# Expert weights of a three-block model, laid out as pairs of tiles and loaded 2 MB at a time in rows of 16 KB

## The chip, the cores and the metric

The kernel runs on one core of a Trainium2 chip. The metric is the device time of one execution in microseconds (us), taken as the median of several runs. A profile of one execution, with a trace of every instruction and of the DMA packets, was taken beside them.

## What is computed

The reference is three transformer-like blocks in a row over one sequence of 256 tokens of width 1024. The change concerns the last part of the third block, a feed-forward of 16 experts in which each expert chooses its 32 tokens:

```python
def expert_choice_ffn(h, w_router, w_gate, w_up, w_down):
    b, s, d = h.shape
    cap = EC_CAPACITY * s // N_EXPERTS          # 2 * 256 // 16 = 32
    affinity = jax.nn.softmax((h @ w_router).astype(jnp.float32), axis=-1)
    top_val, top_idx = lax.top_k(affinity.transpose(0, 2, 1), cap)
    xe = jax.vmap(lambda hb, ib: hb[ib])(h, top_idx)
    act = jax.nn.silu(jnp.einsum('becd,edf->becf', xe, w_gate)) * jnp.einsum('becd,edf->becf', xe, w_up)
    ye = jnp.einsum('becf,efd->becd', act, w_down) * top_val[..., None].astype(h.dtype)
    return jax.vmap(lambda yb, ib: jnp.zeros((s, d), yb.dtype).at[ib.reshape(-1)].add(yb.reshape(-1, d)))(ye, top_idx)
...
        x = x + expert_choice_ffn(rms_norm_3(x, norm_ffn_g[l]), w_router[l], w_exp_gate[l], w_exp_up[l], w_exp_down[l])
    return rms_norm_3(x, norm_final_g)
```

Each expert has a gate and an up matrix of 1024 x 2048 and a down matrix of 2048 x 1024, all float32: 8 MB each, 24 MB per expert, 384 MB in all, and each weight is used for 32 tokens only. The result is summed into the residual and normalized once more.

## The kernel before

Everything is float32 in memory. The first two blocks and most of the third (projections, two kinds of attention, recurrences) run in the first half of the time; their weights come through a ring of three places of 8 KB per partition (`ring`, `load_w`, L282), and each is split into a high and a low part (`wh` on ScalarE and `wl` on VectorE, places in the pool `hl`, `split_w`, L287 to L304) that TensorE multiplies in three products (L311 to L313 and L327 to L329). The residual stands in the pool `res`.

The experts (L1770) work on units of 1 MB: 128 partitions of 8 KB, two tiles of 128 x 1024. A unit of gate or up is 128 rows of the matrix of 2048 columns, so a partition reads one row of 8 KB; a unit of down is 256 rows of 1024 columns, so a partition reads two rows of 4 KB from places half a megabyte apart. `load` (L1876) gives each unit the next of 21 places in turn, issues the transfer on SyncE's queue (SP), and TensorE's matmuls for it follow: four with 512 columns for gate and up (L1902, into the PSUM tile `pgu`), four for down (L1974, into `pd`). The trace shows each such matmul as two instructions, so a unit is a group of 8. The 21 places are, in this order: 13 places in four pools `er0` to `er3` (3, 3, 5 and 2), which are opened one after the other as the third block gives up its memory (`slots`, L246, called at L1729, L1734, L1736 and L1752); the three of `ring`; three in `hl`, where a unit is two transfers of 0.5 MB with rows of 4 KB (`wwh` and `wwl`, L1890); two in `res`. So the first 21 units are on their way while the third block still ends: its last weights w_mg3a and w_mg3b (merging the branches) and w_out3 (output projection) go through the same SP queue, in which the experts' loads stand among them.

Between gate and up and down there are small steps per expert: silu and product (`gg`), four transposes (`pat`, `at`), the weighted one-hot (`pr`, `ppv`, `pvt`), and after down two copies (`ye`) and four matmuls that scatter the result into the residual (`pye`, L1922). The last expert's down is cut by output columns (`parts`: 512, 256, 256), so that norm and output of the first part run beside the loads of the next; its transfers are sixteen of 0.5 MB with rows of 2 KB and 1 KB (L1892). Before the first expert stand the router (L1797 to L1805), softmax, top-k by eight values at a time (L1844 to L1846), and the gathering of tokens by one-hot matmuls (`pxe`, L1861 to L1871), which is interleaved with the first expert's gate and up.

The order of instructions on each engine is set by a scheduling framework that places instructions by their dependences and priorities when the kernel is built; SP issues its transfers strictly in that order and waits at each until its place is free. Eight semaphores serve SP's transfers in turn, so that at most eight are in flight.

Of the kernel before, what the change touches and what calls it, by code (L numbers as in the profile page):

```python
# [10 lines left out]
F32 = mybir.dt.float32  # L11
# [5 lines left out]

S = 256
D = 1024
BIG = 1e30  # L20
EPS = 1e-6

# [141 lines left out]
def layout(x):  # L164
    x = {k: np.asarray(v) for k, v in x.items()}
    a = {}
    ca, coff = const_pack()
    a.update(ca)
    parts = vec_parts(x)
    voff, _ = offsets(parts)  # L170
    a["vecs"] = np.ascontiguousarray(np.concatenate([np.asarray(v, np.float32) for v in parts.values()], 1))
    xt = lambda t: np.ascontiguousarray(t.T.reshape(8, 128, S).transpose(1, 0, 2))
    a["x"] = xt(x["x"][0])
    a["mem"] = xt(x["mem_3"][0])
    a["w_ada"] = np.ascontiguousarray(x["w_ada"][0].T.reshape(12, 2, 128, D).transpose(0, 2, 1, 3)).reshape(12, 128, 2 * D)
    a["crow"] = x["c"]
    w = x["w_in"][0]
    a["w_in"] = wchunks(np.concatenate([w[:, :2048], w[:, 2056:]], 1), 256)
    a["w_ba"] = np.ascontiguousarray(w[:, 2048:2056].reshape(8, 128, 8).transpose(1, 0, 2))
    rows = lambda *names: wchunks(np.concatenate([x[k][0] for k in names], 0), 256)  # L180
    a["w_mg1"] = rows("w_proj_dn", "w_proj_mb")
    a["w_out"] = wchunks(x["w_out"][0], 256)
    w = x["w_in_2"][0]
    a["w_in2"] = wchunks(np.concatenate([w[:, :1536], w[:, 1544:]], 1), 256)
    a["w_if"] = np.ascontiguousarray(w[:, 1536:1544].reshape(8, 128, 8).transpose(1, 0, 2))
    a["lru_w"] = np.ascontiguousarray(np.stack([
        x["lru_wa_2"][0].reshape(2, 128, 64), x["lru_wx_2"][0].reshape(2, 128, 64)], 0).transpose(2, 0, 1, 3))
    a["w_mg2"] = rows("w_out_lru_2", "w_out_mlstm_2", "w_out_sb_2")
    a["w_o2"] = wchunks(x["w_o_2"][0], 256)
    w = x["w_ffn_in_2"][0]  # L190
    a["w_f1"] = np.ascontiguousarray(np.concatenate(
        [w[:, :2816].reshape(1024, 22, 1, 128), w[:, 2816:].reshape(1024, 22, 1, 128)], 2).reshape(1024, 5632))
    a["w_f1"] = wchunks(a["w_f1"], 256)
    w = x["w_ffn_out_2"][0]
    a["w_f2a"] = wchunks(w[:1024], 256)
    a["w_f2b"] = wchunks(w[1024:2048], 256)
    a["w_f2c"] = wchunks(w[2048:], 256)
    a["w_in3"] = wchunks(x["w_in_3"][0], 256)
    pad = np.zeros((6, 7, 127), x["na_rpb_3"].dtype)
    pad[:, :, 48:79] = x["na_rpb_3"][0, :, 4:11]  # L200
    a["rpb"] = np.stack([pad[:, :, 63 - c:127 - c] for c in range(64)], 0)
    a["lora"] = np.ascontiguousarray(np.concatenate([x["rw_w2_3"][0], x["rw_a2_3"][0]], 1).transpose(1, 0, 2))
    a["g2"] = x["rw_g2_3"][0]
    a["w_mkv"] = wchunks(x["w_mem_kv_3"][0], 256)
    a["w_mg3a"] = rows("w_branch_na_3", "w_branch_mem_3")
    a["w_mg3b"] = rows("w_branch_rw_3")
    a["w_out3"] = wchunks(x["w_out_3"][0], 256)
    a["w_rt"] = np.zeros((128, 8, 32), x["w_router_3"].dtype)
    a["w_rt"][:, :, :16] = x["w_router_3"][0].reshape(8, 128, 16).transpose(1, 0, 2)
    a["w_eg"] = x["w_exp_gate_3"][0]  # L210
    a["w_eu"] = x["w_exp_up_3"][0]
    a["w_ed"] = x["w_exp_down_3"][0]
    a["g_fin"] = x["norm_final_g_3"].reshape(1, 1024)
    return {k: np.ascontiguousarray(v) for k, v in a.items()}, coff, voff

ES = [3, 3, 5, 2]
RB = 3  # L220
PB = [3, 3, 2]
HP = None
HB = 3


class Core:
# [19 lines left out]
    def slots(self):  # L246

        n = len(self.er)
        self.er.append(self.ctx.enter_context(self.tc.tile_pool(name=f"er{n}", bufs=ES[n], side="right")))

    def load_vecs(self):
        self.nc.sync.dma_start(self.vt, self.A["vecs"])
# [398 lines left out]
def ada(K, pool):  # L651
# [7 lines left out]
    def part(c0, c1):  # L659
        for c in range(c0, c1):  # L660
            w = K.load_w(K.A["w_ada"][c], 2, D)
            for f in range(2):
# [1107 lines left out]
def experts(K, last, ep, tmp, pool, out):  # L1770

    nc, A, V, C, tc = K.nc, K.A, K.V, K.C, K.tc
# [43 lines left out]
    for t in range(2):  # L1816
        i = nc.scalar.activation(aff[:, t], zl[:, t], AF.Exp, scale=rs[:, t:t + 1], accum_out=su[:, t:t + 1])


    for t in range(2):  # L1820
        for k0 in (0, 4):
            p = K.psum([128, 4, 128], "ptm", "as"[t])
# [5 lines left out]
            else:  # L1828
                with tc.issue_after(i.ins):
                    nc.scalar.copy(d, p)  # L1830
                    nc.scalar.activation(hn[:, t], acc[:, t], AF.Copy, scale=rs[:, t:t + 1])
                    i = nc.scalar.copy(hh[:, t], hn[:, t])
# [37 lines left out]
        else:  # L1870
            nc.vector.tensor_scalar(d, p, V("g_ffn3", k), None, op0=ALU.mult)  # L1871

    slots = [p for p, n in zip(K.er, ES) for _ in range(n)] + [K.ring] * RB + [K.hl] * HB + [K.res] * 2
    cnt = [0]

    def load(src, g=None):  # L1876

        pool = slots[cnt[0] % len(slots)]
        cnt[0] += 1
        if pool is K.hl:  # L1880
            w = [pool.tile([128, 1024], F32, tag=t, name="w" + t) for t in ("wh", "wl")]
        else:
            w = pool.tile([128, 2, 1024], F32, tag="x" if pool is K.res else "w", name="w")
            if g is None:
                nc.sync.dma_start(w, src.rearrange("i p n -> p i n"))
                return w[:, 0], w[:, 1]
            w = w[:, 0], w[:, 1]
        for i in range(2):
            if g is None:
                nc.sync.dma_start(w[i], src[i])  # L1890
            else:
                nc.sync.dma_start(w[i].rearrange("p (g n) -> p g n", g=g), src[i].rearrange("g p n -> p g n"))  # L1892
        return w

    def up(src, e, before=None):
        pg = K.psum([128, 512], "pgu", "g")
        for k in range(8):
            if before is not None:
                before(k)
            w = load(src[e, k * 128:k * 128 + 128, :].rearrange("p (i n) -> i p n", i=2))  # L1900
            for j in range(4):
                nc.tensor.matmul(pg[32 * j:32 * j + 32], xe[:, k, e * 32:e * 32 + 32],  # L1902
                                 w[j // 2][:, j % 2 * 512:j % 2 * 512 + 512], start=k == 0, stop=k == 7)
        return pg
# [6 lines left out]
    def run(work):  # L1911
# [1 line left out]
        gr = work.tile([1, 1024], F32, name="gr")  # L1913
        sm = work.tile([128, 2, 3], F32, name="fsm")
        rs = work.tile([128, 2], F32, name="frs")
        parts = [(0, 512), (512, 768), (768, 1024)]

        def add(pvt, ye, c0, c1):

# [26 lines left out]
        for e in range(16):  # L1946
# [10 lines left out]
            last = nc.scalar.copy(at, pt)  # L1957
# [8 lines left out]
            ye = work.tile([128, 1024], F32, tag="ye", name="ye")  # L1966
            pd = [K.psum([128, 512], f"pd{i}") for i in range(2)]
            if e < 15:
                for c in range(8):
                    w = load(A["w_ed"][e, c * 256:c * 256 + 256, :].rearrange("(i p) n -> i p n", p=128))  # L1970
                    for i in range(2):
                        j, q = divmod(2 * c + i, 4)
                        for hh in range(2):
                            nc.tensor.matmul(pd[hh][32 * q:32 * q + 32], at[:, q, 32 * j:32 * j + 32],  # L1974
                                             w[i][:, hh * 512:hh * 512 + 512], start=j == 0, stop=j == 3)
                nc.scalar.copy(ye[:, 0:512], pd[0])  # L1976
                nc.vector.tensor_copy(ye[:, 512:1024], pd[1])  # L1977
                for c0 in (0, 512):
                    for _ in add(pvt, ye, c0, c0 + 512):
                        pass  # L1980
                continue
# [6 lines left out]
            for n, (c0, c1) in enumerate(parts):  # L1988
                m = c1 - c0
                g = 1024 // m  # L1990
                p = pd[c0 // 512][:, c0 % 512:c0 % 512 + m]
                for i in range(0, 16, 2 * g):
                    w = load(A["w_ed"][e, i * 128:(i + 2 * g) * 128, c0:c1].rearrange("(i g p) n -> i g p n", i=2, g=g), g)
                    for u in range(2 * g):
                        j, q = divmod(i + u, 4)
                        nc.tensor.matmul(p[32 * q:32 * q + 32], at[:, q, 32 * j:32 * j + 32],
                                         w[u // g][:, u % g * m:u % g * m + m], start=j == 0, stop=j == 3)
                h = c0 + m // 2
                nc.scalar.copy(ye[:, c0:h], p[:, 0:m // 2])
                nc.vector.tensor_copy(ye[:, h:c1], p[:, m // 2:])  # L2000
                for t, a in add(pvt, ye, c0, c1):
                    finish(t, n, a)
# [7 lines left out]
def body(ctx: ExitStack, tc: tile.TileContext, A, out, coff, voff):  # L2010
    nc = tc.nc
    K = Core(ctx, tc, A, coff, voff)
# [12 lines left out]
    with tc.tile_pool(name="b3", bufs=1) as pool:  # L2025
        last = block3(K, xt, pool, mem, norms)
        ep = ctx.enter_context(tc.tile_pool(name="ep", bufs=1, side="right"))
        with tc.tile_pool(name="et", bufs=1) as tmp:
            run = experts(K, last, ep, tmp, pool, out)
    with tc.tile_pool(name="ew", bufs=1) as work:  # L2030
        run(work)
    K.late.close()

# [14 lines left out]
```

## Time and profile before

| | |
|---|---|
| median of 3 runs | 1981.33 us (1977.47 to 1982.41) |
| the profiled execution | 1979.57 us |
| its span, first to last instruction | 1977.6 us |
| TensorE (PE), VectorE (DVE), ScalarE (ACT), GpSimd (POOL) busy | 1649.7, 771.7, 590.2, 106.8 us |
| DMA over the span | 557.04 MB in 106917 packets, mean 282 GB/s |
| the chain that ended last | PE 46%, DMA 41%, DVE 8% of the span |

The page of a profile gives busy time by engine, the span in 40 slices of 49.4 us with one digit per slice for the busy share in tenths, the rate of DMA in each slice, the chain of work that ended last (followed back from the last instruction through what released each step), the costliest groups of instructions, and the transfers. The trace answers narrower questions: tables of busy time by stretches, the waits of an engine and what ended them, and instructions in order of time. GB are 10^9 bytes; a MB of a weight unit is 2^20 bytes.

### The profile page before, as it was taken

The numbers are of one execution on the slowest core, as the hardware profiler recorded it, in microseconds if no ns is written. First come the engines' busy times: TensorE is split into PE (matmuls) and PEld (weight loads), VectorE is DVE, ScalarE is ACT, GpSimd is POOL, SyncE is SP. The second block draws the span as 40 slices with busy tenths as digits, with TensorE's granted clock in tenths as the row PEclk, the third lists the DMA queues.
The fourth block names the chain that finished last, engine by engine and source line by source line (L and its number), as shares of the span: only waits on it lengthen the run. The fifth ranks groups of instructions, "written<-read, shape, count | busy, mean of one in ns | idle before, by whom it ended". The sixth has DMA issues, their size and how long they took to land.

```text
span 1977.6 us, 28659 instructions
## 1 busy us (share of the span) xinstructions
PE 1649.7 (83%) x11882; PEld 1062.5 (54%) x11882; DVE 771.7 (39%) x1529; ACT 590.2 (30%) x1159; POOL 106.8 (5%) x123
## 2 busy tenths in 40 slices
PE   3999989999999999989979776677777677767776
PEld 2998989899999998868974111111111111111111
DVE  7797767657655676855571000000000000000001
ACT  3655555764554454633441000000000000000001
POOL 0000000000000121300020000000000000000000
PEclk9998989999999999979999888888878889777888
DMA  7442643344545553322689999999999999999998
GB/s 298 171 149 89 230 170 117 138 141 173 177 174 186 179 198 128 108 76 88 235 310 375 414 415 415 415 417 416 416 416 415 416 416 414 414 415 417 418 416 293
DMA packets 106917, 557.04 MB, mean 282 GB/s; under 512 B 10530, under 2 KB 17058, under 8 KB 61859
## 3 DMA queue, kind: packets, MB, share of 16 engines
q1 hardware_dynamic: 106786, 555.21, 72.1%
q8 instruction: 93, 1.52, 0.3%
q14 instruction: 38, 0.30, 0.0%
HBM read 554.12 MB, written 1.05 MB: 281 GB/s over the span
## 4 chain that ended last, share of the span: by engine, by line
PE 46%; DMA 41%; DVE 8%; ACT 2%; issue 1%; SPq 1%; POOL 1%; DVEq 0%; ACTq 0%
DMA w<-in_w_eg 15%; DMA w<-in_w_eu 13%; PE psg L313 10%; PE psg L311 10%; PE psg L312 10%; DMA w<-in_w_ed 5%; DMA wwl<-in_w_eu 4%; DVE wl L302 2%; PE pgu L1902 2%; PE pd L1974 2%; DMA wwh<-in_w_eu 1%; DVE w L664 1%; DMA wwl<-in_w_eg 1%; DMA wwh<-in_w_eg 1%; PE psg L328 1%
## 5 line engine op out<-in xcount | busy, mean ns | idle before, releaser
L1902 PE MATMUL pgu<-w,xe 128*32 128x512 f32 x1768 | 304.2, 782 | 155.1 <-DMA w<-in_w_eu 89.1
L302 DVE TENSOR_TENSOR wl<-w,wh 128x512 fp32r<-128x512 f32 (+1 forms) x510 | 330.6, 690 | 183.2 <-ACT wh L300 170.6
L300 ACT CAST wh<-w 128x512 fp32r<-128x512 f32 x516 | 287.7, 607 | 253.1 <-PE psg L312 223.3
L1902 PEld LDWEIGHTS pgu<-w,xe 128*32 128x32 f32 x1768 | 42.9, 121 | 393.6 <-DMA w<-in_w_eu 222.3
L1974 PE MATMUL pd<-w,at 128*32 128x512 f32 x808 | 186.0, 637 | 48.5 <-DMA w<-in_w_ed 43.0
L1952 DVE TENSOR_TENSOR gg<-gg,pgu 128x512 f32<-128x512 f32 x16 | 11.0, 688 | 503.9 <-PE pgu L1902 500.3
L1974 PEld LDWEIGHTS pd<-w,at 128*32 128x32 f32 x808 | 42.2, 115 | 183.5 <-DMA w<-in_w_ed 112.7
L1977 DVE COPY ye<-pd 128x512 f32<-128x512 f32 x15 | 10.4, 692 | 294.5 <-PE pd L1974 294.5
L313 PE MATMUL psg<-n3hh,wl 128*128 128x256 f32 x344 | 103.0, 299 | 3.2 <-POOL wl L302 1.7
L311 PE MATMUL psg<-h1h,wh 128*128 128x256 f32 x352 | 103.0, 293 | 0.0
L311 PE MATMUL psg<-n3hh,wh 128*128 128x256 f32 x344 | 101.5, 295 | 1.6 <-ACT wh L300 1.6
L313 PE MATMUL psg<-h1h,wl 128*128 128x256 f32 x352 | 102.2, 290 | 0.0
L312 PE MATMUL psg<-h1l,wh 128*128 128x256 f32 x352 | 101.7, 289 | 0.0
L1957 ACT COPY at<-pat 128x512 f32<-128x512 f32 x16 | 9.4, 585 | 308.6 <-PE pat L1955 297.1
L312 PE MATMUL psg<-n3hl,wh 128*128 128x256 f32 x344 | 100.8, 293 | 0.1
L312 PE MATMUL psg<-n2fhl,wh 128*128 128x256 f32 x352 | 100.0, 284 | 0.2
L313 PE MATMUL psg<-n2fhh,wl 128*128 128x256 f32 x352 | 99.8, 283 | 0.0
L311 PE MATMUL psg<-n2fhh,wh 128*128 128x256 f32 x352 | 99.6, 283 | 0.0
L1951 ACT ACTIVATE gg<-pgu 128x512 f32<-128x512 f32 x16 | 9.6, 597 | 277.3 <-PE pgu L1902 277.2
L311 PE MATMUL psg<-n2hh,wh 128*128 128x256 f32 x304 | 87.1, 287 | 2.0 <-ACT n2hh L453 2.0
L312 PE MATMUL psg<-n2hl,wh 128*128 128x256 f32 x304 | 87.7, 289 | 0.2 <-DVE n2hl L456 0.2
L1976 ACT COPY ye<-pd 128x512 f32<-128x512 f32 x15 | 8.8, 585 | 264.6 <-issue 257.3
(725 smaller groups left out, 3473.8 us busy)
## 6 DMA issues: line engine op xcount, KB each, us to landing
w<-in_w_eg SPq DMA_DIRECT2D x112, 1024.0 KB, 18.5
w<-in_w_eu SPq DMA_DIRECT2D x109, 1024.0 KB, 19.9
w<-in_w_ed SPq DMA_DIRECT2D x101, 1024.0 KB, 18.8
w<-in_w_in SPq DMA_DIRECT2D x68, 1024.0 KB, 4.8
w<-in_w_f SPq DMA_DIRECT2D x22, 1024.0 KB, 4.8
w<-in_w_ada SPq DMA_DIRECT2D x12, 1024.0 KB, 5.3
wwh<-in_w_ed SPq DMA_DIRECT2D x19, 512.0 KB, 14.7
wwl<-in_w_ed SPq DMA_DIRECT2D x19, 512.0 KB, 15.2
```

The lines of the kernel that those rows point to most:

```text
L300: self.nc.scalar.copy(wh[:, a:b], w[:, k0 + a:k0 + b])
L302: e.tensor_tensor(wl[:, a:b], w[:, k0 + a:k0 + b], wh[:, a:b], op=ALU.subtract)
L311: nc.tensor.matmul(out, a, x[0], start=first, stop=False)
L312: nc.tensor.matmul(out, a, x[1], start=False, stop=False)
L313: nc.tensor.matmul(out, b, x[0], start=False, stop=last)
L328: nc.tensor.matmul(out, xl[:, k, ts], wh[:, c0:c1], start=False, stop=False)
L664: nc.vector.scalar_tensor_tensor(w[:, f], w[:, f], 1.0, sg, op0=ALU.mult, op1=ALU.mult, accum_out=out[:, j:j + 1])
L1902: nc.tensor.matmul(pg[32 * j:32 * j + 32], xe[:, k, e * 32:e * 32 + 32], w[j // 2][:, j % 2 * 512:j % 2 * 512 + 512], start=k == 0, stop=k ...
L1951: nc.scalar.activation(gg, pgu[0], AF.Silu)
L1952: nc.vector.tensor_tensor(gg, gg, pgu[1], op=ALU.mult)
L1974: nc.tensor.matmul(pd[hh][32 * q:32 * q + 32], at[:, q, 32 * j:32 * j + 32], w[i][:, hh * 512:hh * 512 + 512], start=j == 0, stop=j == 3)
L1977: nc.vector.tensor_copy(ye[:, 512:1024], pd[1])
```

## The change

The host lays the expert weights out anew. Gate and up become blocks of 256 matrix rows in which each partition's two rows of 8 KB follow each other; down becomes blocks of 512 matrix rows in which each partition's four rows of 4 KB follow each other. A block is 2 MB, 16 KB per partition in one piece. The last expert's down is stored apart (`w_edl`), in eight blocks of 1 MB in the order in which its column parts use them, 8 KB per partition in one piece.

The places become eight of 16 KB and four of 8 KB, 20 MB: six pairs and one single in the `er` pools (whose sizes change from 3, 3, 5, 2 to 2, 4, 4, 3), the three singles of `ring`, and two pairs in a new pool `lw`, which is opened where `hl` and `res` stood, once both are closed (K.late.close() moves ahead of the experts' main part). A pair's place takes a block in one transfer with rows of 16 KB; two single places take a block in two transfers with rows of 8 KB. The matmuls are the same, in the same units. `load` becomes a generator that hands out one unit after the other.

```diff
+LAST = [(0, 512), (512, 768), (768, 1024)]
...
-    a["w_eg"] = x["w_exp_gate_3"][0]
-    a["w_eu"] = x["w_exp_up_3"][0]
-    a["w_ed"] = x["w_exp_down_3"][0]
+    for k, n in (("w_eg", "w_exp_gate_3"), ("w_eu", "w_exp_up_3")):
+        a[k] = x[n][0].reshape(16, 4, 2, 128, 2048).transpose(0, 1, 3, 2, 4)
+    w = x["w_exp_down_3"][0]
+    a["w_ed"] = w.reshape(16, 4, 4, 128, 1024).transpose(0, 1, 3, 2, 4).reshape(16, 4, 128, 2, 2048)
+    last = []
+    for c0, c1 in LAST:
+        g = 1024 // (c1 - c0)
+        last.append(w[15, :, c0:c1].reshape(8 // g, 2 * g, 128, c1 - c0).transpose(0, 2, 1, 3).reshape(8 // g, 128, 2048))
+    a["w_ed"] = a["w_ed"][:15]
+    a["w_edl"] = np.concatenate(last, 0)
...
-ES = [3, 3, 5, 2]
+ES = [2, 4, 4, 3]
...
-        self.er.append(self.ctx.enter_context(self.tc.tile_pool(name=f"er{n}", bufs=ES[n], side="right")))
+        if ES[n] % 2:
+            self.er1 = self.ctx.enter_context(self.tc.tile_pool(name="er", bufs=1, side="right"))
+        self.er.append(self.ctx.enter_context(self.tc.tile_pool(name=f"er{n}", bufs=ES[n] // 2, side="right")))
...
-    slots = [p for p, n in zip(K.er, ES) for _ in range(n)] + [K.ring] * RB + [K.hl] * HB + [K.res] * 2
+    slots = [(p, 2) for p, n in zip(K.er, ES) for _ in range(n // 2)] + [(K.er1, 1)] + [(K.ring, 1)] * RB + [(None, 2)] * 2
     cnt = [0]
 
-    def load(src, g=None):
...
+    def load(srcs):
+
+        for src in srcs:
+            two, i = len(src.shape) == 3, 0
+            while i < (2 if two else 1):
+                pool, n = slots[cnt[0] % len(slots)]
+                cnt[0] += 1
+                pool = pool or K.lw
+                if n == 2:
+                    w = pool.tile([128, 2, 2048], F32, tag="w2", name="w")
+                    assert i == 0
+                    if two:
+                        nc.sync.dma_start(w, src)
+                    else:
+                        nc.sync.dma_start(w[:, 0], src)
+                else:
+                    w = pool.tile([128, 1, 2048], F32, tag="w", name="w")
+                    nc.sync.dma_start(w[:, 0], src[:, i] if two else src)
+                for q in range(min(n, 2 if two else 1)):
+                    yield w[:, q, 0:1024], w[:, q, 1024:2048]
+                    i += 1
...
-            w = load(src[e, k * 128:k * 128 + 128, :].rearrange("p (i n) -> i p n", i=2))
+            w = next(ws)
...
-                    w = load(A["w_ed"][e, c * 256:c * 256 + 256, :].rearrange("(i p) n -> i p n", p=128))
+                    w = next(ws)
...
-                    w = load(A["w_ed"][e, i * 128:(i + 2 * g) * 128, c0:c1].rearrange("(i g p) n -> i g p n", i=2, g=g), g)
+                    w = next(load([A["w_edl"][next(edl)]]))
...
+    K.late.close()
+    K.lw = ctx.enter_context(tc.tile_pool(name="lw", bufs=2))
     with tc.tile_pool(name="ew", bufs=1) as work:
         run(work)
-    K.late.close()
```

How this moves the transfers on SP's queue is told by the built programs, at three places. First, the end of the third block, where SP's queue has the experts' first loads among the last weights of the block (w_mg3a, w_mg3b, w_out: 640, 384 and 1024 KB each; 128x2048 is 1 MB, 128x4096 is 2 MB). Before:

```order
L1885 DMA w<-in_w_eg 128x2048 x6
L284 DMA w<-in_w_mg3a 128x1280
L1885 DMA w<-in_w_eg 128x2048 x2
L284 DMA w<-in_w_mg3a 128x1280
L1885 DMA w<-in_w_eu 128x2048
L284 DMA w<-in_w_mg3a 128x1280
L1885 DMA w<-in_w_eu 128x2048
L284 DMA w<-in_w_mg3b 128x768 x2
L1885 DMA w<-in_w_eu 128x2048
L284 DMA w<-in_w_mg3b 128x768 x2
L284 DMA w<-in_w_out 128x2048 x3
L257 DMA ct_b3e<-in_consts_b3e 128x96
```

The same stretch of SP's queue in the changed kernel:

```order
L1899 DMA w<-in_w_eg 128x4096 x2
L294 DMA w<-in_w_mg3a 128x1280
L1899 DMA w<-in_w_eg 128x4096
L294 DMA w<-in_w_mg3a 128x1280 x2
L1899 DMA w<-in_w_eg 128x4096
L294 DMA w<-in_w_mg3b 128x768 x3
L1899 DMA w<-in_w_eu 128x4096
L294 DMA w<-in_w_mg3b 128x768
L294 DMA w<-in_w_out 128x2048 x2
L267 DMA ct_b3e<-in_consts_b3e 128x96
L1786 DMA wr<-in_w_rt 128x256
L294 DMA w<-in_w_out 128x2048 x2
```

A pair now stands ahead of the last w_mg3b, the two constants (`ct_b3e`, `wr`) stand ahead of the third w_out instead of behind it, and the fourth w_out follows the third at once. Second, behind this on the same queue, the places are filled for the first time and then go round. Before:

```order
L1885 DMA w<-in_w_eu 128x2048
L284 DMA w<-in_w_out 128x2048
L1885 DMA w<-in_w_eu 128x2048 x3
L1890 DMA wwh<-in_w_ed 128x1024
L1885 DMA w<-in_w_eu 128x2048
L1890 DMA wwl<-in_w_ed 128x1024
...
L1885 DMA w<-in_w_ed 128x2x1024 x5
L1885 DMA w<-in_w_eg 128x2048 x8
L1885 DMA w<-in_w_eu 128x2048 x5
```

In the changed kernel:

```order
L1899 DMA w<-in_w_eu 128x4096
L1904 DMA w<-in_w_eu 128x2048 x4
L1899 DMA w<-in_w_ed 128x4096 x4
L1899 DMA w<-in_w_eg 128x4096 x4
L1904 DMA w<-in_w_eu 128x2048 x4
```

The first two w_ed pairs go to `lw`, the next two are the first that reuse a place; from there on every twenty units are eight transfers of 2 MB and four of 1 MB. Third, the end of SP's queue, the last expert's up and down. Before:

```order
L1885 DMA w<-in_w_eu 128x2048 x5
L1890 DMA wwh<-in_w_eu 128x1024
...
L1890 DMA wwl<-in_w_eu 128x1024
L1892 DMA w<-in_w_ed 128x2x512 x8
L1892 DMA w<-in_w_ed 128x4x256 x8
L1941 DMA out<-acc 128x512
```

In the changed kernel:

```order
L1899 DMA w<-in_w_eu 128x4096 x2
L1904 DMA w<-in_w_eu 128x2048 x4
L1901 DMA w<-in_w_edl 128x2048 x8
L1957 DMA out<-acc 128x512
```

Sixteen transfers of 0.5 MB have become eight of 1 MB.

## Rows read from the trace of the kernel before

**Rows 1.** The page, part 2: the span in 40 slices, busy tenths of DMA and its rate.

```profile
DMA  7442643344545553322689999999999999999998
GB/s 298 171 149 89 230 170 117 138 141 173 177 174 186 179 198 128 108 76 88 235 310 375 414 415 415 415 417 416 416 416 415 416 416 414 414 415 417 418 416 293
DMA packets 106917, 557.04 MB, mean 282 GB/s; under 512 B 10530, under 2 KB 17058, under 8 KB 61859
```

**Rows 2.** Expert stage: stretch, length, busy PE, PEld, DVE, ACT, POOL, clock, DMA share, GB/s.

```profile
1050.00:1950.00 900.00, 663.91 (x3218) 145.41 (x3214) 64.61 (x95) 37.29 (x71) 18.87 (x32) 0.86 1.02 415
```

**Rows 3.** Waits of SP's queue, 1050 to 1950 us: total us, times, longest us.

```profile
SPq L1885 <- DMA w<-in_w_eg: 137.9, 67, 2.1
...
SPq L1885 <- PE pgu L1902: 59.0, 40, 4.5
...
SPq L1885 <- PE pd L1974: 23.4, 20, 4.5
```

**Rows 4.** The page, part 6: transfers, count, KB each, median us from issue to landing.

```profile
w<-in_w_ed SPq DMA_DIRECT2D x101, 1024.0 KB, 18.8
```

**Rows 5.** The table by stretches around the end of the third block, columns as above.

```profile
1035.00:1040.00 5.00, 2.69 (x14) 2.27 (x18) 3.46 (x6) 0.18 (x1) 1.28 (x1) 0.50 0.11 45
1040.00:1045.00 5.00, 5.00 (x42) 1.97 (x34) 0.48 (x1) 0.77 (x2) 0.00 (x0) 0.90 0.49 145
```

**Rows 6.** The chain that ended last, 980 to 1060 us: start, us, engine, tile, line.

```profile
1000.77 0.67 DVE mgl L391 x2
...
1004.27 0.12 PE psg L312
...
1027.45 0.70 ACT aff L1817 x4
...
1039.72 2.50 PE pgu L1902 x16
1042.22 1.36 PE pxe L1866 x10
```

**Rows 7.** The same chain, 1900 us to the end.

```profile
1944.42 1.08 PE pgu L1902 x4
...
1966.95 0.68 PE pd L1996 x8
```

**Rows 8.** PE in order of time, 1094 to 1140 us: units of down (start, us, count, idle before).

```profile
1100.75 1.92 PE L1974 MATMUL pd<-w,at 128*32 128x512 f32 x8 [0.64 <-DMA w<-in_w_ed]
...
1113.52 1.92 PE L1974 MATMUL pd<-w,at 128*32 128x512 f32 x8 [0.62 <-DMA w<-in_w_ed]
```

**Rows 9.** The same view: units of gate and up.

```profile
1119.79 2.78 PE L1902 MATMUL pgu<-w,xe 128*32 128x512 f32 x24
1123.50 1.07 PE L1902 MATMUL pgu<-w,xe 128*32 128x512 f32 x8 [0.93 <-DMA w<-in_w_eg]
...
1138.45 1.81 PE L1902 MATMUL pgu<-w,xe 128*32 128x512 f32 x8 [0.54 <-DMA w<-in_w_eu]
```

**Rows 10.** SP's queue in order of time, 1041 to 1044 us.

```profile
1041.44 1.23 SPq L1885 DMA_DIRECT2D w<-in_w_ed  x2
```

**Rows 11.** SP's queue in order of time, 980 to 1050 us.

```profile
1000.25 0.33 SPq L257 DMA_DIRECT2D ct_b3e<-in_consts_b3e  x1
...
1001.51 0.33 SPq L1885 DMA_DIRECT2D w<-in_w_eu  x1
1003.28 0.33 SPq L284 DMA_DIRECT2D w<-in_w_out  x1
```

**Rows 12.** Waits of all engines, 950 to 1060 us: total us, times, longest.

```profile
ACT wh L300 <- DMA w<-in_w_out: 1.3, 1, 1.3
```

**Rows 13.** PE in order of time, 1937 to 1942 us: units in the places of `hl`.

```profile
1939.29 1.05 PE L1902 MATMUL pgu<-wwl,xe 128*32 128x512 f32 x4 [0.23 <-DMA wwl<-in_w_eu]
1940.57 1.05 PE L1902 MATMUL pgu<-wwh,xe 128*32 128x512 f32 x4 [0.23 <-DMA wwh<-in_w_eu]
```

**Rows 14.** The page, part 3: DMA queue, packets, MB, share of 16 engines over the span.

```profile
q8 instruction: 93, 1.52, 0.3%
```

More of the change, by code (lines that the diff above doesn't have):

```diff
@@ L1871, in gather @@
             nc.vector.tensor_scalar(d, p, V("g_ffn3", k), None, op0=ALU.mult)
-    slots = [p for p, n in zip(K.er, ES) for _ in range(n)] + [K.ring] * RB + [K.hl] * HB + [K.res] * 2
+    slots = [(p, 2) for p, n in zip(K.er, ES) for _ in range(n // 2)] + [(K.er1, 1)] + [(K.ring, 1)] * RB + [(None, 2)] * 2
     cnt = [0]
-    def load(src, g=None):
[L1878 to L1893, printed above, removed]
+    def load(srcs):
[18 more added lines that the diff above has]
+                    i += 1
     def up(src, e, before=None):
         pg = K.psum([128, 512], "pgu", "g")
+        ws = load([src[e, c] for c in range(4)])
         for k in range(8):
@@ L1915, in run @@
         rs = work.tile([128, 2], F32, name="frs")
-        parts = [(0, 512), (512, 768), (768, 1024)]
+        parts = LAST
+        edl = iter(range(8))
         def add(pvt, ye, c0, c1):
@@ L1968, in run @@
             if e < 15:
+                ws = load([A["w_ed"][e, c] for c in range(4)])
                 for c in range(8):
-                    w = load(A["w_ed"][e, c * 256:c * 256 + 256, :].rearrange("(i p) n -> i p n", p=128))
+                    w = next(ws)
                     for i in range(2):
```

## The prediction

> **What bounds the kernel now.** Start with the page: its 40 slices say that from the 23rd on, 1088 us, the DMA engines are busy without a break at 414 to 418 GB/s [rows 1]. That second half is the expert feed-forward, which reads 384 MB of weights. Next the table by stretches: over 900 us of it, DMA has a share of 1.02 at 415 GB/s, TensorE is busy for 664 us, VectorE for 65, ScalarE for 37 [rows 2]. So the stage lasts as long as its bytes take. The waits of the DMA queue (SP) say why it never runs dry: SP waits mostly for earlier weight transfers to land (it keeps eight in flight), and for TensorE's use of a place only 59.0 and 23.4 us, 4.5 at the longest [rows 3], with the transfers issued 18.8 us (median) before they land [rows 4]. A place that comes free late therefore costs nothing there.
>
> Ahead of the stage is one hole. DMA has a share of only 0.11 from 1035 to 1040 us and of 0.49 from 1040 to 1045 [rows 5]: nothing moves from about 1036.5 to 1042.5. All 21 places of 1 MB are full, and the first comes free when TensorE has used the first weights, for which the router, top-k and gather have to finish (chain: softmax, top-k, gather, then the first group of pgu from 1039.72) [rows 6]. After the last weights land at 1966.9 another 10.7 us of reduction, norm and output follow [rows 7]. So the end is: end of the hole, plus the remaining megabytes times the time of one, plus a tail.
>
> **The change, part by part.** *Time of a megabyte.* In the stage TensorE starts a unit as soon as it lands, so the starts of its groups are a clock. Down-weights come in rows of 4 KB: six starts from 1100.75 to 1113.52 make 12.77/5 = 2.554 us for 1 MB [rows 8]. Gate and up come in rows of 8 KB: seven starts from 1123.50 to 1138.45 make 14.95/6 = 2.492 us [rows 9]. Each of the 16 DMA engines has 16 rows of a megabyte in the first case and 8 in the second, so a row costs (2.554 - 2.492)/8 = 0.00775 us beside its bytes. With 16 KB rows an engine has 4, and I extrapolate 2.492 - 4 x 0.00775 = 2.461 us, an estimate from these two rows. Its bounds: 2.492 if a longer row brings nothing more, 2.430 if it costs nothing at all. I take 2.461 because it is the straight line through what is measured; for 16 KB rows of weights no row exists.
>
> *The units, before.* By the code 21 are loaded ahead of the hole, 363 after it: 205 in 8 KB rows (gate and up, but for the three `hl` places of 21), 150 in 4 KB rows (all of down for experts 0 to 14, and the `hl` places), and the last expert's 8 in rows of 2 and 1 KB, which take from 1944.42 to 1966.95, 22.5 us [rows 7]. Sum: 205 x 2.492 + 150 x 2.554 + 22.5 = 510.9 + 383.1 + 22.5 = 916.5 us. The trace has 1966.9 - 1042.5 = 924.4, so 7.9 us (0.9%) are not in my sum; I leave them as they are.
>
> *The units, after.* The places hold six pairs, four singles and two pairs: 20 MB, one fewer, so 364 follow the hole. 284 of them are in 16 KB rows; 80 are in 8 KB rows (four of every twenty, and the last eight). Sum: 284 x 2.461 + 80 x 2.492 = 698.9 + 199.4 = 898.3. The difference is -18.2 us, the megabyte lost from the places (2.5 us) included; 2.6 of it is the last expert.
>
> The Trainium skill speaks against this much: DMA: Bandwidth & Descriptors, section "Why small descriptors are slow (HBM only)", gives a fixed overhead of about 3 cycles per packet of 32-byte beats and finds joining descriptors worth it only at 256 B or less. By that 4 KB rows would cost 1.2% more than 8 KB rows (131/128 against 259/256), where the rows above show 2.5%; worked through the same units it is an estimate of -7.0 us in place of -18.2. The measured rows decide, and that the rule is nearer is the second rival.
>
> *Hole.* Before, the first place of 1 MB is free for an issue at 1041.44 [rows 10]. A pair is free when both its units are used, and the second one's matmuls end at 1042.22 [rows 6]: **+0.8**. The two new `lw` pairs lie where `hl` and the residual stood, so the first waits for TensorE's and ScalarE's last reads of it, at the latest until 1028.1 (aff) [rows 6]. The pairs would land by about 1028.1 + 2 + 2 x 4.9 = 1040, still ahead of 1042, so that costs nothing; if the cover went, it would be the 2 us or so by which they are late.
>
> *Queue order before the hole.* SP is in order, and 2 MB pairs now stand in it between the merge's and output projection's weights: a pair (4.9 us of transfer) ahead of the last w_mg3b, where 1 MB stood two loads earlier; and the two small constants, which waited for the merge until 1000.25 [rows 11], now go ahead of the third w_out instead of behind it. That w_out is issued at 1000.6 rather than about 997, but TensorE has 48 matmuls of 0.12 us [rows 6] for each of its four chunks and is through the merge only after 1001, so the third is not needed before about 1012. The fourth no longer stands behind an expert's megabyte (it did, 1001.51 before 1003.28 [rows 11]), but it was waited for only 1.3 us [rows 12]. The last w_mg3b may land about 3 us later, in a stretch that VectorE's and ScalarE's splitting bounds [rows 6]. Bounds -1.3 and +3; I take **+1.0**, nearer to the middle than to the 3, since that load had some 2 us in hand.
>
> *Tail.* The last 0.5 MB needs 8 matmul instructions, 0.68 us [rows 7]; the last load is now a whole megabyte with 16: **+0.7**. What follows it is unchanged.
>
> *Nothing:* half as many issues on SP (it only waits), the unchanged number of matmuls. TensorE must keep up with 59 us per expert (24 x 2.461): the long groups of a unit take 1.92 us [rows 8], so 24 take about 46 us, plus two joints per expert, of which the one after down takes 4.4 us (from 1113.52 + 1.92 [rows 8] to 1119.79 [rows 9]): some 55 us at the worst. Hidden, with 4 us in hand.
>
> Sum: -18.2 + 0.8 + 1.0 + 0.7 = **-15.7 us**. Against the profiled execution's 1979.57 us (span 1977.6 and 2.0 around it) that is 1963.9; the median of the three runs is 1.8 above that execution, so 1965 to 1966. I say **1965 us**.
>
> **The rivals.** *16 KB rows go no faster than 8 KB rows* (moved in pieces of 8 KB or less, or another limit reached; this is also the case in which the change doesn't do what it says). The 4 KB rows still become 8 KB. 284 x 0.031 = 8.8 us are lost: -6.9, 1972.7 and with the 1.8 about 1974. For it: no weight row in this trace is longer than 8 KB. Against: 4 to 8 KB showed no flattening, and the last expert's 2 and 1 KB rows lie on the same line (4 x 2.678 + 4 x 2.926 = 22.4 us by it, 22.5 measured). 0.13.
>
> *Only half of the difference is the rows' own*: the rest belongs to what is read (down-weights, two pieces to a tile) and stays. Rate saving without the lost megabyte is 20.7; half is 10.3: -15.7 + 10.3 = -5.4, about 1976: no change (0.3%, 5.9 us, is about what a measurement of this kernel can tell). Against: the `hl` halves of gate and up were 4 KB rows too, and step by 1.28 us for 0.5 MB [rows 13], as slow as down-weights. 0.08. The Trainium skill's 3 cycles, above, would come out near here.
>
> *A 16 KB row costs more than two of 8 KB* (memory side: each engine now stays four times as long in one place, and rows are 16 KB apart). No gain at 284x = 698.9 + 15.7, x = 2.516 us per MB, only 1% over 8 KB rows; slower by over 0.3% from 2.537. At the 2.554 of 4 KB rows it gives 284 x 0.093 = +26.4, so +10.7 or 1992 us. For it: the only 16 KB packets in the trace, 93 of instructions, took 0.3% of 16 engines' time, about 1 us each [rows 14], against 0.62 for two 8 KB rows (2 x 2.492/8). Against: those shared engines with the weights, and rows have only gained by length. 0.07. (The Trainium skill, DMA: Bandwidth & Descriptors, section "Latency and other measured facts", has rows at a pitch of 2 MiB and more lose a fifth and more; no run here shows it, and the pitch here is 16 KB.)
>
> *The places hold the queue up*: 20 MB in larger places, freed two at a time, with up to 16 MB in flight. The stream breaks only if TensorE is late by more than is in flight, 12 MB or 29 us at the least; the longest wait for it is 4.5 [rows 3]. In the hand-over a late merge or router could cost 10 us. Then -5, 1976. 0.06.
>
> **How the numbers follow.** Forecast 0.66; rivals 0.13, 0.08, 0.07, 0.06. Faster by over 0.3%: the forecast and two thirds of the first rival, 0.74. Within 0.3%: the rest of it, the second and the last, 0.19. Slower: 0.07. The forecast's own bounds are -15.7 - 8.8 - 2.3 and -15.7 + 8.8 + 2; the range from 1955 to 1978 takes in nearly all of these and the rivals but the third.
>
> **What would show it.** In the profile after: the stage's rate at 424 to 427 GB/s instead of 415; starts of TensorE's pair groups 4.92 us apart; a packet count near 60,000 rather than 106,917; the hole longer by 1 to 3 us, beginning later than 1039; SP still waiting for landings rather than for pgu. Steps of 4.98 would mean the first rival; 5.03 and more the third; DMA slices under 9 after the hole the fourth. The prediction is wrong if the rate is under 420 GB/s, or the hole ends after 1047.

## The result and the profile after

The changed kernel takes 1961.16 us (median of 4 runs, 1955.69 to 1964.23); the kernel before, timed beside it, 1979.82 (4 runs, 1977.47 to 1982.41). The ratio is 0.9908, 95% interval 0.9893 to 0.9923. 1965 was predicted, in a range from 1955 to 1978. The profiled execution is the slowest of the four: 1964.23 us, span 1962.1, 15.5 less than the span of before.

The page of the changed kernel, its DMA slices of 49.1 us, their rates, and the packets, against [rows 1]:

```profile
DMA  8442543344455554320488999999999999999997
GB/s 300 157 156 97 215 163 134 130 146 159 176 188 173 180 194 171 107 79 25 178 328 342 426 427 425 426 426 426 426 426 425 426 426 426 426 426 424 427 426 316
DMA packets 59361, 556.99 MB, mean 284 GB/s; under 512 B 7138, under 2 KB 9570, under 8 KB 12643
```

From the 23rd slice to the 39th the rate is 424 to 427 GB/s, and the same bytes go in 59,361 packets. The table by stretches, with the columns of [rows 2]:

```profile
1050.00:1930.00 880.00, 567.57 (x3236) 140.16 (x3228) 64.86 (x96) 35.35 (x68) 18.88 (x32) 0.83 1.01 426
1030.00:1035.00 5.00, 3.03 (x27) 2.33 (x22) 3.68 (x12) 3.14 (x9) 0.00 (x0) 1.00 0.33 66
...
1040.00:1045.00 5.00, 2.88 (x14) 2.27 (x18) 3.27 (x6) 0.37 (x1) 1.09 (x1) 0.50 0.87 370
1045.00:1050.00 5.00, 5.00 (x34) 1.92 (x30) 0.48 (x1) 0.57 (x2) 0.00 (x0) 0.72 0.30 56
```

The stage is bound by its bytes as before. The hole [rows 5] has become three smaller ones: by the packets nothing but a few instructions moves from 1002.8 to 1005.8, from 1030.2 to 1033.7 (the first `lw` pair waits for its place) and from 1045.3 to 1049.1. SP's queue in order of time, 1035 to 1058 us, has the first load into a place used before at 1048.10, which was 1041.44 [rows 10]:

```profile
1048.10 3.54 SPq L1899 DMA_DIRECT2D w<-in_w_ed  x2
```

TensorE in order of time, 1094 to 1142 us: pairs of down, then single units of gate (start, us, count, idle before):

```profile
1111.02 1.95 PE L1991 MATMUL pd<-w,at 128*32 128x512 f32 x16 [1.28 <-DMA w<-in_w_ed]
1115.92 3.58 PE L1991 MATMUL pd<-w,at 128*32 128x512 f32 x16 [2.95 <-DMA w<-in_w_ed]
1120.83 1.95 PE L1991 MATMUL pd<-w,at 128*32 128x512 f32 x16 [1.33 <-DMA w<-in_w_ed]
...
1135.62 1.07 PE L1917 MATMUL pgu<-w,xe 128*32 128x512 f32 x8 [1.43 <-DMA w<-in_w_eg]
1138.10 1.07 PE L1917 MATMUL pgu<-w,xe 128*32 128x512 f32 x8 [1.42 <-DMA w<-in_w_eg]
1140.58 1.93 PE L1917 MATMUL pgu<-w,xe 128*32 128x512 f32 x8 [1.42 <-DMA w<-in_w_eg]
```

A pair starts every 4.90 us (9.81/2), a megabyte of down every 2.45 instead of 2.554 [rows 8]; singles in 8 KB rows every 2.48, near the 2.492 of [rows 9]. The waits of SP's queue, 1050 to 1930 us, with the columns of [rows 3]:

```profile
SPq L1899 <- DMA w<-in_w_ed: 158.9, 48, 4.9
SPq L1899 <- DMA w<-in_w_eg: 134.1, 43, 5.0
...
SPq L1904 <- DMA w<-in_w_eg: 107.8, 24, 4.6
```

SP still waits for landings; its longest single wait for TensorE is 5.4 us (pd). The chain that ended last, the hand-over and the end, against [rows 6, 7]:

```profile
1032.26 0.70 ACT aff L1827 x4
...
1044.53 3.50 PE pgu L1917 x16
1048.03 1.37 PE pxe L1876 x10
...
1931.43 1.57 PE pgu L1917 x8
...
1935.38 3.71 PE pgf L2003 x4
1939.08 5.14 PE pd L2013 x32
...
1950.86 1.93 PE pd L2013 x32
```

**Where the 15.5 us come from**, profile against profile, in pieces that follow one another (packet times worked out from the DMA packets of the trace):

| piece | before | after | difference |
|---|---|---|---|
| start to the issue of the first w_mg3a | 911.1 | 914.3 | +3.2 |
| to the end of softmax (aff) | 117.0 | 118.6 | +1.6 |
| to the first reuse of a place | 13.3 | 15.2 | +1.9 |
| to the last weight packet | 925.0 | 903.1 | -21.9 |
| to the end of the span | 11.2 | 10.9 | -0.3 |

The third piece is +0.9 for a pair instead of a single and +1.0 because the first group of pgu took 3.50 us instead of 2.50: granted clock 0.72 in this stretch, 0.90 before [rows 5]. The first piece lies in instructions that the change doesn't touch: in the first 911 us both kernels execute the same ones. Whether it is chance is open. In the three profiled executions of the change the first w_mg3a was issued at 912.2 to 914.3, before at 911.1, and in those of the eight other variants below, again with the same instructions up to there, at 905.6 to 909.9. So the times and ratios below can hold some 5 us that have nothing to do with a variant's loads, and next to each time stands the stretch **from the issue of the first w_mg3a to the last weight packet**: 1055.4 us before, 1036.9 in the change, a difference of 18.5.

### The profile page after: what moved, and what is told of

The parts are those of the page before. It is cut to its first block, busy times and chain, and to the rows that moved or that the text cites. A ratio compares the mean times of both kernels' runs of the same rounds, so it can differ in the third digit from the quotient of the medians.

```text
span 1962.1 us, 28246 instructions
## 1 busy us (share of the span) xinstructions
PE 1556.5 (79%) x11882; PEld 1059.4 (54%) x11882; DVE 773.6 (39%) x1529; ACT 590.0 (30%) x1159; POOL 106.6 (5%) x123
## 2 busy tenths in 40 slices
DMA packets 59361, 556.99 MB, mean 284 GB/s; under 512 B 7138, under 2 KB 9570, under 8 KB 12643
## 4 chain that ended last, share of the span: by engine, by line
PE 45%; DMA 44%; DVE 7%; ACT 2%; issue 1%; POOL 1%; SPq 0%; DVEq 0%; ACTq 0%
DMA w<-in_w_eu 15%; DMA w<-in_w_ed 15%; DMA w<-in_w_eg 13%; PE psg L323 11%; PE psg L321 10%; PE psg L322 10%; DVE wl L312 2%; PE pgu L1917 1%; DMA w<-in_w_ada 1%; DVE w L674 1%; PE atps L491 1%; PE psg L338 1%; PE psg L337 1%; PE psg L339 1%; PE pxe L1876 1%
## 5 line engine op out<-in xcount | busy, mean ns | idle before, releaser
L1917 PE MATMUL pgu<-w,xe 128*32 128x512 f32 x2048 | 317.0, 736 | 205.5 <-DMA w<-in_w_eu 124.4
L1917 PEld LDWEIGHTS pgu<-w,xe 128*32 128x32 f32 x2048 | 59.9, 122 | 444.3 <-DMA w<-in_w_eu 210.9
L1991 PE MATMUL pd<-w,at 128*32 128x512 f32 x960 | 173.2, 773 | 85.8 <-DMA w<-in_w_ed 81.1
L323 PE MATMUL psg<-n2hh,wl 128*128 128x256 f32 x304 | 87.1, 287 | 0.0
```

The costliest lines, as they stand in the source:

```text
L323: nc.tensor.matmul(out, b, x[0], start=False, stop=last)
```

## The experiments

The theory: what is gained is a fixed cost per row of a transfer, paid for fewer rows. Rivals: the transfer's size (2 MB instead of 1), the contiguous piece read in memory, the number of places or the queue's depth. Where a time between landings is given, it is the median of the steps from one transfer's last semaphore update to the next one's, 1060 to 1930 us: 4.901 us for a pair in the change, 2.483 for a single, and before 2.492 for a megabyte in 8 KB rows and 2.560 in 4 KB rows.

**Rows of 8 KB in transfers of 2 MB** (x1). The two megabytes of a pair lie apart in memory again:

```diff
-        a[k] = x[n][0].reshape(16, 4, 2, 128, 2048).transpose(0, 1, 3, 2, 4)
+        a[k] = x[n][0].reshape(16, 4, 2, 128, 2048)
...
-                        nc.sync.dma_start(w, src)
+                        nc.sync.dma_start(w, src.rearrange("i p n -> p i n"))
...
```

The layout of down and the loads of single places change in the same way.

> Same places and same 2 MB transfers as the change, but the two units of a block lie 1 MB apart in memory, so that a transfer moves rows of 8 KB. Theory (the time of a megabyte is its bytes plus a fixed cost per row): pairs step by 2 x 2.49 = 4.98 us instead of the change's 4.90, about 15,000 packets more, and the kernel is 284 x 0.04 = 11 us slower than the change, about 0.997 of before. Rival (fewer and larger transfers made the gain): pairs step by 4.90 as in the change, and the kernel is as fast as the change, 0.991.

Measured: 1970.16 us (10 runs, 1968.16 to 1973.05), ratio 0.9954 (0.9937 to 0.9970); the stretch 1048.0. The packets, and TensorE on pairs of down, in order of time:

```profile
DMA packets 78560, 556.99 MB, mean 283 GB/s; under 512 B 7137, under 2 KB 9569, under 8 KB 12642
```

```profile
1103.00 1.95 PE L1991 MATMUL pd<-w,at 128*32 128x512 f32 x16 [1.44 <-DMA w<-in_w_ed]
1107.98 3.27 PE L1991 MATMUL pd<-w,at 128*32 128x512 f32 x16 [3.03 <-DMA w<-in_w_ed]
1112.96 1.95 PE L1991 MATMUL pd<-w,at 128*32 128x512 f32 x16 [1.72 <-DMA w<-in_w_ed]
```

Steps of 4.98 here (4.980 as the median of the landings), 2.490 us a megabyte: in transfers of 2 MB 8 KB rows cost what they cost before in transfers of 1 MB (2.492). Of the 18.5 us in the stretch 11.1 are gone with the rows (11 were expected), and the transfer's size gives next to nothing.

**Rows of 4 KB** (x3), the same places and transfers; the host stores tiles of 128 x 1024, half a megabyte apart, and single places are loaded in the same way:

```diff
...
-                        nc.sync.dma_start(w, src)
+                        nc.sync.dma_start(w.rearrange("p a (b n) -> p (a b) n", b=2), src.rearrange("i p n -> p i n"))
...
```

> The change with rows of 4 KB everywhere but in the last expert's down (four tiles of 128 x 1024 per block, half a megabyte apart in memory), same places and 2 MB transfers. Theory (fixed cost per row, 0.0078 us on each engine): pairs step by 2 x 2.554 = 5.11 us, the stage's rate falls to 410 GB/s, and the kernel is 356 units x about 0.1 = 34 us slower than the change, about 1.008 of before. Rival (size of a transfer): as fast as the change.

Measured: 1994.04 us (6 runs, 1991.62 to 2000.9), ratio 1.0075 (1.0050 to 1.0099); the stretch 1072.3; 409 GB/s in 126,688 packets, 5.120 us a pair and 2.560 a megabyte (median of the landings), as down had before. With rows of 4 KB the change would have made the kernel slower; gate and up are now as slow as down (5.120 for each of the three), so the cost belongs to the row, not to the matrix.

**One piece in memory, two rows in SBUF** (x4). The layout of the change, with a gap of 64 B between the halves of a pair's place:

```diff
-                    w = pool.tile([128, 2, 2048], F32, tag="w2", name="w")
+                    w = pool.tile([128, 2, 2064], F32, tag="w2", name="w")
...
-                        nc.sync.dma_start(w, src)
+                        nc.sync.dma_start(w[:, :, 0:2048], src)
...
```

> The change's memory layout, 16 KB in one piece per partition, but the place in SBUF has a gap of 64 bytes between its two units, so that a transfer has to be cut into rows of 8 KB although it reads the same addresses in the same order. Theory (cost per row moved): pairs step by 4.98 us and the kernel is 11 us slower than the change, as with the units 1 MB apart. Rival (what counts is that the memory is read in long pieces): 4.90 us, as fast as the change. If the packets of the trace are still 16 KB, it tells nothing.

Measured: 1969.98 us (7 runs, 1968.26 to 1973.38), ratio 0.9955 (0.9933 to 0.9976); the stretch 1047.3. The trace has 78,560 packets, as many as with the units apart in memory, so the rows were cut into 8 KB. The table by stretches:

```profile
1100.00:1900.00 800.00, 507.13 (x2759) 116.65 (x2752) 55.12 (x80) 28.01 (x55) 15.41 (x26) 0.81 1.01 422
```

Pairs land 4.968 us apart, against 4.980 where their units also lie apart in memory and 4.901 in the change. So what counts is the piece that is moved as one, on both sides: it is worth 0.067 us per pair, and that memory is read in order 0.012 at most.

**Rows of 32 KB** (x5). The two last pairs become one place of 32 KB, filled in one transfer of 4 MB; gate, up and down are laid out so that a partition's rows of a matrix all follow each other:

```diff
...
-    slots = [(p, 2) for p, n in zip(K.er, ES) for _ in range(n // 2)] + [(K.er1, 1)] + [(K.ring, 1)] * RB + [(None, 2)] * 2
+    slots = [(p, 2) for p, n in zip(K.er, ES) for _ in range(n // 2)] + [(K.er1, 1)] + [(K.ring, 1)] * RB + [(None, 4)]
...
+            nc.sync.dma_start(w[:, 0:k], src[:, u:u + k])
...
```

> The change with the two places of lw joined to one of 32 KB per partition: every twentieth megabyte starts a transfer of 4 MB in rows of 32 KB. Each matrix is laid out with its eight units behind each other in a partition, so rows of all lengths stand 64 KB apart. Theory (fixed cost per row, now 0.0087 us by the steps 2.557, 2.486, 2.451 of 4, 8 and 16 KB rows): a 4 MB transfer takes 4 x 2.433 = 9.73 us against 9.80 for two pairs; 73 such units give 1.3 us, under what a time can tell, so the step decides. Rival (a limit near 16 KB): 9.80. Rival (distance of the rows in memory counts): pairs and singles step by clearly more than 4.90 and 2.49, and the kernel is slower than the change.

Measured: 1957.36 us (4 runs, 1954.78 to 1959.28), ratio 0.9899 (0.9879 to 0.9920); the stretch 1035.8. 4 MB land in 9.729 us, 2.432 a megabyte; pairs of 16 KB rows, which now stand 64 KB apart in memory, still in 4.90. The four lengths lie close to one line:

| row | rows per engine and MB | us per MB | less for each row saved |
|---|---|---|---|
| 4 KB (x3) | 16 | 2.560 | |
| 8 KB, apart in memory (x1) | 8 | 2.490 | 0.0088 from x3 |
| 8 KB, together in memory (x4) | 8 | 2.484 | |
| 16 KB (the change) | 4 | 2.4505 | 0.0084 from x4, 0.0099 from x1 |
| 32 KB (x5) | 2 | 2.432 | 0.0091 |

The first three lengths are in transfers of 2 MB, the last in one of 4 MB.

**The same rows in transfers of 1 MB** (x2), meant to tell rows from transfers the other way round:

```diff
-                        nc.sync.dma_start(w, src)
+                        for p0 in (0, 64):
+                            nc.sync.dma_start(w[p0:p0 + 64], src[p0:p0 + 64])
```

> The change with each pair's transfer cut in two of 1 MB, partitions 0 to 63 and 64 to 127, rows of 16 KB as in the change. Theory (rows): a pair still takes 4.90 us, and the kernel is as fast as the change, 0.991 of before, within 3 us. Rival (size of a transfer): 1 MB transfers go at the 2.49 us of before's, and the kernel is 11 us slower than the change. A third way: each half reaches only some of the DMA engines evenly, and the rate falls clearly.

Measured: 2791.06 us (2776 to 2798), ratio 1.4079 (1.4019 to 1.4138). The table by stretches:

```profile
1100.00:2700.00 1600.00, 698.43 (x2924) 154.37 (x2924) 61.32 (x89) 29.20 (x57) 15.42 (x26) 0.62 1.01 225
```

The DMA share is 1.01 and the rate 225 GB/s: the engines count as busy throughout, and a 16 KB packet takes 1186 ns in the mean instead of 616. So this run tells nothing on the transfer's size; what it shows is that transfers into 64 partitions move at about half the rate, and that the next in the queue doesn't fill the other half. The Trainium skill, SBUF — State Buffer, section "Door 1: The DMA port swizzle (why `[64,N]` ≈ `[32,N]`)", has partitions 0 to 63 reach only 8 of 16 ports; its 27.2 GB/s per port make an estimate of 218 GB/s. The same page of the Trainium skill, section "Can I just issue two DMAs to hit both halves?", says that two transfers aren't fused to reach all ports. The trace is near both: 225, with a fifth of the bytes still going into 128 partitions.

**Fewer places in the kernel before** (x6): 16 of 1 MB, without those in `hl` and `res`:

```diff
-    slots = [p for p, n in zip(K.er, ES) for _ in range(n)] + [K.ring] * RB + [K.hl] * HB + [K.res] * 2
+    slots = [p for p, n in zip(K.er, ES) for _ in range(n)] + [K.ring] * RB
```

> The kernel before without the places in hl and res: 16 places instead of 21, all loads of 1 MB. Theory (a place is worth one megabyte's time, since all places are full when the first expert starts): 5 x 2.5 = 12.5 us more behind the hole, less about 35 units of gate and up that go from rows of 4 KB to 8 KB (-2.3): 10 us slower than before, 1.005, with the stage's rate unchanged or 1 GB/s higher. Rival (the number of places matters for the queue's depth): the DMA engines show gaps in the stage, its rate falls, and the kernel is slower by more than 15 us.

Measured: 1987.69 us (6 runs, 1984.01 to 1993.42), ratio 1.0052 (1.0033 to 1.0071); the stretch 1066.7, +11.3. The table by stretches:

```profile
1100.00:1900.00 800.00, 569.03 (x2724) 117.05 (x2724) 54.34 (x79) 27.42 (x54) 15.41 (x26) 0.81 1.02 416
```

The rate stays (416 GB/s). By the packets the hole lasts 19.2 us (1023.0 to 1042.2) instead of 5.9, 13.2 more or about a megabyte's time for each of the five places; some 2 us come back, about what the expectation gave to units that go from 4 KB rows to 8 KB rows. Places matter as what can be loaded before the hole, not as depth of the queue.

**One more place, used once** (x8), 8 KB in a pool behind `lw`, for the 21st unit:

```diff
...
+                if two and cnt[0] == len(slots) and not K.extra:
+                    K.extra = True
+                    w = K.lx.tile([128, 1, 2048], F32, tag="w", name="w")
+                    nc.sync.dma_start(w[:, 0], src[:, 0])
...
```

> The change with one more place of 8 KB, used once: hl and res leave 40 KB, lw takes 32, and the 21st megabyte goes to the other 8 before the first place is free. Theory (what is loaded before the first expert starts is bounded by the places, and each megabyte loaded there is 2.45 us less behind it): the last idle stretch of the DMA queue, 1.5 to 3 us before the first place comes free, is filled, and the kernel is 1.5 to 2.5 us faster than the change, 0.990 of before. Rival (the loads into the former hl and res come too late for more): the hole ends later by as much, no gain.

Measured: 1956.47 us (4 runs, 1953.68 to 1960.97), ratio 0.9902 (0.9874 to 0.9929). The stretch is 1035.0, 1.9 less than in the change: the last gap shrinks from 2.7 us without a packet (1045.3 to 1046.3 and 1047.3 to 1049.1, with one of instructions between) to 0.6 (1040.7 to 1041.3). The time alone doesn't tell it from the change.

**The change again** (x0), to see how much of the hand-over belongs to one execution:

> The change once more, unaltered, for a second profile. If the 4.8 us by which its first profile reached the first expert's gate late (1.4 of it in the merge, 3.4 before 300 us) belong to the change's order on the DMA queue, they come back; if they are the execution's own, the hole of the DMA engines ends between 1040 and 1045 as in the two kernels with rows of 8 KB, which have the same order. Ratio to before 0.991 within 0.002 either way; pairs step by 4.90 us.

Measured: 1961.55 us (4 runs, 1959.1 to 1965.71), ratio 0.9924 (0.9901 to 0.9946); the stretch 1036.95. The hole didn't end at 1040 to 1045 but at 1048.6, since the first w_mg3a was issued late again, at 913.8; from there to the start of the last aff 118.75 us against 118.45. So the lateness came back, which by the expectation speaks for the kernel rather than for one execution; but it arises ahead of the first load that the change moves.

**Both additions** (x9: 32 KB place and extra place) and, timed beside it, the change (x10):

> The change with both additions: the last two pairs joined to one place of 32 KB (4 MB transfers), and one more place of 8 KB that is used once, for the first megabyte behind the 20. If rows and places act apart from one another, the savings add: from the issue of the first w_mg3a to the landing of the last weight 1036.9 - 1.1 - 1.9 = 1033.9 us, against 1036.9 in the change, 1035.8 with the 32 KB place alone and 1035.0 with the extra megabyte alone; the time then some 3 us below the change, 0.989 to 0.991 of the kernel before. Rival: the extra megabyte shifts the units against the places, a pair's place is filled by half and the 4 MB place comes due earlier, so that one saving eats the other: 1035 to 1036 us, and no difference from either alone.

> The change unaltered, on the same chip and in the same rounds as the version with both additions. Its median is expected at 1960 to 1963 us; the version with both additions should lie 2 to 4 us below it if the savings add, within 1 us of it if one eats the other.

Measured: 1952.66 us (4 runs, 1950.67 to 1955.19), ratio 0.9876 (0.9857 to 0.9895), and for the change 1959.3 (6 runs, 1957.84 to 1966.92), 0.9915 (0.9895 to 0.9935). The stretch is 1033.0 against 1037.1: the two savings add. This version beats both kernels, the change by 6.6 us, of which the stretch accounts for 4.1. In the profiles the rest lies ahead of it: the first w_mg3a was issued at 906.2 against 912.2. The table by stretches, 165 to 170 us, first of the change in x10, then of the version with both:

```profile
165.00:170.00 5.00, 5.00 (x31) 4.66 (x31) 1.40 (x4) 1.08 (x3) 0.00 (x0) 0.50 0.30 126
```

```profile
165.00:170.00 5.00, 5.00 (x52) 4.93 (x51) 3.92 (x14) 1.57 (x6) 0.00 (x0) 1.00 0.36 147
```

TensorE's granted clock there is 0.50, the 1.2 GHz level, in one and 1.00 in the other; what ran just before it are small matmuls of 32 x 32 among those of 128 x 128. The version with both additions is past this place some 4 us earlier. It was 0.50 in before and in all three profiled executions of the change, and 1.00 in the eight other variants, whose instructions up to there are the same. Why, no run tells, and the 3.2 us between before and the change aren't explained by it, since both have 0.50 there. A difference of a few us between variants can come from this place, so it has to be read in the stretch.

## Why the prediction was right

Its mechanism holds: bytes plus a fixed cost per row. By its steps:

*Time of a megabyte.* 2.461 us were estimated for 16 KB rows, 2.4505 measured, inside the bounds of 2.492 and 2.430. The saving over 8 KB rows was mis-sized: 0.031 us estimated, 0.0415 measured, and 284 megabytes make 3.0 us more gain out of it. The row's cost, 0.00775 us, rested on five steps of 4 KB rows at 2.554; over the whole stage of the same trace their median is 2.560, which gives 0.0085 a row and 2.458. The rest stays open: singles in 8 KB rows, too, land 0.009 us sooner in the change than before, with rows of equal length.

*The sum over the stage.* Predicted -18.2, measured -21.9: the 3.0 above, and 0.7 from 80 singles at 2.483 instead of 2.492. What the sum leaves out stayed the same: 925.0 - 916.5 = 8.5 us before; 284 x 2.4505 + 80 x 2.483 = 894.6, and 903.1 - 894.6 = 8.5 after.

*Hole.* +0.8 predicted for the pair, +0.9 measured. Not foreseen is the 1.0 of the lower clock in the first group of pgu. The first `lw` pair finds its place late (the gap from 1030.2 to 1033.7), and that costs nothing, as predicted: the second has landed at 1045.6, 2.5 us ahead of the first reuse.

*Queue order.* +1.0 taken, +1.6 measured between first w_mg3a and aff (118.45 to 118.75 us to the start of the last aff in eight of the nine executions in that order that were compared, 116.86 before). The last w_mg3b lands 83.9 us after the first w_mg3a's issue instead of 80.0, a little more than the 3 us that were foreseen, and ct_b3e, which waits for the merge, is issued 1.3 us later. But the kernel before with 16 places has 117.80, so up to 0.9 of the 1.6 may not be the order's. The order alone wasn't tried.

*Tail.* +0.7 predicted, -0.3 between the two profiles, which is no measure of the term. It asks that TensorE waits for the last load, and in the profiled change it doesn't: the chain ends in its own work, from the last up-unit at 1931.43 on, and its last 32 matmuls start at 1950.86, before the last packet at 1951.2. The faster stream alone doesn't explain that, since in x4 and x9 TensorE waits for the last load as before. What differs is how much of the work ahead fell into the lower clock: in the change it was 0.50 from 1935 to 1940 us, and pgf took 3.71 us, against 1.96 before and some 2.5 in x9. The stretch in the change, pgf before, and in x9 the 16 matmuls that wait for the last load:

```profile
1935.00:1940.00 5.00, 5.00 (x14) 1.49 (x16) 0.00 (x0) 3.31 (x5) 0.00 (x0) 0.50 1.01 419
```

```profile
1947.21 1.96 PE pgf L1986 x4
```

```profile
1939.65 1.07 PE L2010 MATMUL pd<-w,at 128*32 128x256 f32 x16 [0.58 <-DMA w<-in_w_edl]
```

Where TensorE does wait, in x4 and x9, the scatter (pye) behind these 16 starts 2.26 and 2.24 us after the last packet, against 1.84 before: +0.4 of the +0.7. That the whole tail isn't longer is because what follows this scatter's start took 9.35 us in the profile of before and 8.6 to 8.8 in all others. In the change itself the end of the span came 10.9, 12.8 and 11.1 us after the last packet in its three profiled executions.

So the terms came to -21.9 + 1.9 + 1.6 - 0.3 = -18.7, and the profiled execution gave 3.2 back ahead of all of it, in instructions that the change doesn't touch. That its -15.5 lies next to the predicted -15.7 is luck: the two errors nearly cancel. The medians differ by 18.7 us, as the terms do; in the two later comparisons, x0 and x10, by 15.4 and 18.1.

*Its own signs.* The rate (426), the step of pairs (4.90 for 4.92), the packets (59,361) and SP's waits came as it said. The hole didn't: it was to grow by 1 to 3 us and begin after 1039, and there were three gaps of 3.0, 3.5 and 3.8 us, the first at 1002.8. And the prediction called itself wrong if the hole ends after 1047; it ended at 1049.1. The first place is reused 6.7 us later than before, 3.5 by the two terms above and 3.2 by what lies ahead of them; the sign was counted from the start of the execution and so took in those 3.2.

*The rivals.* The first, no gain beyond 8 KB, would have had steps of 4.98; that is x1, not the change. The second, half of the difference, falls with x3 and x4: gate, up and down cost the same at equal rows. The third falls with 616 ns for a 16 KB packet against twice 314 for 8 KB ones. Of the fourth there is no sign in the waits of SP or in the slices behind the hole. The 3 cycles per packet of the Trainium skill (DMA: Bandwidth & Descriptors, section "Why small descriptors are slow (HBM only)") are too few here: 3/259 of an 8 KB row's 0.311 us is an estimate of 3.6 ns, against 8.4 to 9.9 measured.

## What to carry to other kernels

When a stage lasts as long as its bytes and the transfers queue up deep enough, count the rows: each cost 8 to 10 ns of a DMA engine here, from 4 KB rows up to 32 KB. So lay weights out on the host so that one partition's share of a transfer is one piece in memory and in SBUF, and leave the number of places for what can be loaded ahead of a hole. Read the step between landings in the trace of before at two row lengths, over the whole stage rather than from a few steps, and follow the row that ends the chain: with a faster stream or a lower granted clock it can be an engine's own work.

## What the runs showed of the hardware unexpectedly

- Into 64 partitions the DMA engines, at a share of 1.01, moved 225 GB/s, against 426 into 128.
- The gain doesn't flatten up to 32 KB: 0.0084 to 0.0099 us for each row saved, and rows 64 KB apart in memory land as fast as rows 16 KB apart (4.90 us a pair).
- In equal instructions TensorE's granted clock was 0.50 in some profiled executions and 1.00 in others from 165 to 170 us, worth some 4 us there.
